# Feature tiles 32 bytes further on their line each, and the weights' parts in six separate buffers at different places

## The chip, the cores and the metric

One core of one Trainium2 chip runs the whole kernel. The metric is device time in microseconds: 953.28 us, the median of three runs (951.79, 953.28, 955.75). The engines are named as in the profile: PE multiplies matrices, PEld is its loading of the stationary operand, DVE and ACT are the vector and the scalar engine, SP issues the DMAs. Arrays lie in the on-chip memory with 128 partitions; an address below is a byte offset within a partition, the same in all partitions.

## The reference

One layer of a hybrid decoder trunk, for one sequence of 256 tokens and 2048 features (D), with a branch width of 4096 (E), all in float32:

```python
h = rmsnorm(x, norm_g);  mod = silu(c) @ ada_w + ada_b      # shift, scale, gate: 3 x 2048
h = h * (1 + scale) + shift
b, c_gate, v, g = split(h @ w_in, 4)                        # w_in: 2048 x 16384
u = causal_depthwise_conv(c_gate * v, conv_w)               # 3 taps
y = b * u * silu(g)
x = x + gate * (y @ w_out)                                  # w_out: 4096 x 2048
out = rmsnorm(x, final_g)
```

Nearly all the arithmetic is in `h @ w_in` (128 MiB of weights) and `y @ w_out` (32 MiB); `silu(c) @ ada_w` reads another 48 MiB.

## The kernel before, in words

**Two parts of each number.** A float32 product is made of three products of a shorter format (fp32r). Both operands are split: hi is the value rounded by ACT's cast (L191), lo is the rest, subtracted by DVE (L192). `split` (L187) does this for each raw block of weights that a DMA brings. A raw block, a hi block and a lo block take 8192 bytes of a partition each (SLOT = 2048 numbers), and each kind has three buffers that its pool hands out in turn. The tokens' features are split likewise: hT holds for each of 16 feature tiles k a row of 512 numbers, 256 tokens hi (`hh_`) and 256 tokens lo (`hl_`).

**Part 1 (`part`, L264; to about 406 us of the profile).** The first half of the branch channels, in four chunks by four quarters of w_in. While the conditioning vector's shift and scale are still being computed (`ada_piece`, L216, on DVE), matmuls begin with the feature tiles that are finished; `plan` (L41) sets that order, and a scheduler then places the instructions of all engines. For each feature tile k and each of four 128-channel columns there are three matmuls of 256 token columns: weights hi with features hi (L286), hi with lo (L291), lo with hi (L292). Each has its own load of stationary weights, a 128x128 block, so 3072 matmuls and 3072 loads. 85 blocks are split here.

**Part 2 (L365, about 407 to 762 us).** The second half: per feature tile and column one matmul of 512 columns (L382: weights hi with features hi and lo side by side) and one of 256 (L385: weights lo with features hi); 1024 of each, 64 blocks.

**Part 3 (L449, about 763 to 943 us).** y @ w_out. Now y is stationary (128 tokens of one channel tile, y hi or y lo) and the weights of w_out move, 512 columns: L427 (y hi, weights hi), L428 (y hi, weights lo), L429 (y lo, weights hi); 768 matmuls, 32 blocks. In the last quarter of the output, dc = 3, the matmuls of the second half of the tokens, po[1], with the last three blocks are put behind all of po[0] (the list `late`, L473 and L498), and the tail of the first half of the tokens (`gated`, L477, `finish`, L433: square, root, scale, store) runs beside them.

**Order of loads and matmuls on PE.** A matmul's stationary block is loaded while the matmul before it runs. So each matmul of the three parts reads its moving tile while the next matmul's weights are read from another place of the same memory.

**Small buffers.** The first group of ada_w pieces (four pieces, `at0`, L226) borrows two lo and two hi buffers. `gjunk` (L211, 512 bytes) takes the unused output of 32 small ACT sums (L249).

Of the kernel before, what the change touches and what calls it, by code (L numbers as in the profile page):

```python
# [8 lines left out]
F32 = mybir.dt.float32  # L9
F32R = mybir.dt.float32r  # L10
AF = mybir.ActivationFunctionType
ALU = mybir.AluOpType

P = 128
D = 2048
E = 4096
T = 256
KT = D // P
# [17 lines left out]
SLOT = 2048  # L36
ASLOT = 1024
# [51 lines left out]
def short_conv_layer(ctx: ExitStack, tc: tile.TileContext, x, c, norm_g, ada_w, ada_b, w_in, conv_w, w_out, final_g, out):  # L89
    nc = tc.nc  # L90
    PSUM = bass.MemoryType.PSUM

    const = ctx.enter_context(tc.tile_pool(name="const", bufs=1))
    adap = ctx.enter_context(tc.tile_pool(name="adap", bufs=2))
    wpool = ctx.enter_context(tc.tile_pool(name="wpool", bufs=2))
    psum = ctx.enter_context(tc.tile_pool(name="psum", bufs=6, space=PSUM))
    hpool = ctx.enter_context(tc.tile_pool(name="hpool", bufs=1, side="right"))
# [65 lines left out]

    hT = hpool.tile([P, KT, 2 * T], F32R, tag="big", name="hT")
    hh_ = hT[:, :, 0:T]
    hl_ = hT[:, :, T : 2 * T]
    xs = [slot([P, CT, T], f"xs{j}") for j in range(KT // CT)]
# [1 line left out]
    for k in range(0, KT, 2):  # L171
        tp = psum.tile([P, 2, T], F32, tag="sm", name="tp_x", bufs=2)
# [11 lines left out]
    shift = const.tile([P, KT], F32, tag="shift", name="shift")  # L184
    scale = const.tile([P, KT], F32, tag="scale", name="scale")

    def split(raw, n):  # L187

        hi = wpool.tile([P, SLOT], F32R, tag="hi", name="hi", bufs=3)
        lo = wpool.tile([P, SLOT], F32R, tag="lo", name="lo", bufs=3)  # L190
        nc.scalar.copy(hi[:, :n], raw[:, :n])  # L191
        nc.vector.tensor_tensor(out=lo[:, :n], in0=raw[:, :n], in1=hi[:, :n].bitcast(F32), op=ALU.subtract)  # L192
        return hi, lo
# [14 lines left out]


    acc = {}  # L210
    gjunk = const.tile([P, P], F32, tag="gjunk", name="gjunk")  # L211
    adas = ada_w[0].rearrange("(k p) (s f) -> p k s f", p=P, s=3)

    sums = {}
# [1 line left out]
    def ada_piece(k0, nk, piece):  # L216
        w = nk * P
        kk = ASLOT // (2 * w)
        if piece == 0:
            sums[k0] = adap.tile([P, 2, 2 * P], F32, tag="gv", name="gv")  # L220
        gv = sums[k0]

        turns = [gv[:, :, i * w : (i + 1) * w] for i in range(2 if k0 == 0 and nk == 1 else 1)]
        j = piece * kk
        if k0 == 0:
            at = wpool.tile([P, SLOT], F32, tag=("lo", "hi")[piece % 2], name="at0", bufs=3)[:, :ASLOT]  # L226
        else:
            at = adap.tile([P, ASLOT], F32, tag="at", name="at", bufs=4)
        at4 = at.rearrange("p (k s f) -> p k s f", k=kk, s=2)
        for s in range(2):  # L230
            nc.sync.dma_start(at4[:, :, s, :], adas[:, j : j + kk, s, k0 * P : k0 * P + w])  # L231
        for i in range(kk):
            c_k = silu_c[:, j + i : j + i + 1]
            g2 = turns[(j + i) % len(turns)]
            if j + i < len(turns):
                nc.vector.tensor_scalar_mul(g2, at4[:, i], c_k)
            else:
                nc.vector.scalar_tensor_tensor(out=g2, in0=at4[:, i], scalar=c_k, in1=g2, op0=ALU.mult, op1=ALU.add)  # L238
        if j + kk < KT:
            return  # L240
        if len(turns) == 2:
            nc.vector.tensor_tensor(out=turns[0], in0=turns[0], in1=turns[1], op=ALU.add)

        tp = psum.tile([P, 4, P], F32, tag="sm", name="tp_g", bufs=2)
        gs = const.tile([P, 4], F32, tag="gs", name="gs", bufs=2)
        for o in range(2 * nk):
            nc.tensor.transpose(tp[:, o, :], gv[:, o // nk, (o % nk) * P : (o % nk + 1) * P], ident)
        for o in range(2 * nk):
            nc.scalar.activation(gjunk, tp[:, o, :], AF.Copy, accum_out=gs[:, o : o + 1])  # L249
        ks = slice(k0, k0 + nk)  # L250
        nc.vector.tensor_tensor(out=scale[:, ks], in0=gs[:, nk : 2 * nk], in1=b_scale[:, ks], op=ALU.add)
        nc.vector.tensor_tensor(out=shift[:, ks], in0=gs[:, 0:nk], in1=b_shift[:, ks], op=ALU.add)
        nc.vector.scalar_tensor_tensor(
            out=scale[:, ks], in0=scale[:, ks], scalar=1.0, in1=gT[:, ks], op0=ALU.add, op1=ALU.mult
        )
        for k in range(k0, k0 + nk):
            hf = xs[k // CT][:, k % CT, :]
            nc.vector.tensor_scalar(
                out=hf, in0=hf, scalar1=scale[:, k : k + 1], scalar2=shift[:, k : k + 1], op0=ALU.mult, op1=ALU.add
            )  # L260
            nc.scalar.copy(hh_[:, k], hf)  # L261
            nc.vector.tensor_tensor(out=hl_[:, k], in0=hf, in1=hh_[:, k].bitcast(F32), op=ALU.subtract)
# [55 lines left out]
    for kind, *step in plan():  # L318
        if kind == "ada":
            ada_piece(*step)  # L320
        else:
            ch, k1 = step[0], step[3]
            part(*step)
            whole[ch] += k1 == KT
            if k1 == KT and whole[ch] == 4:
                mixed(ch)
# [40 lines left out]
    for ct in range(NS, NCT, 2):  # L367
        for q in QUARTERS:
            banks = [psum.tile([P, 2, T], F32, tag="mm", name="mm_b") for _ in range(2)]
            col = q * E + ct * P  # L370
            for kp in range(0, KT, KP):
# [5 lines left out]
                hi, lo = split(raw, SLOT)  # L377
                for m in range(2):
                    for i in range(KP):
                        k = kp + i  # L380
                        o = slice((i * 2 + m) * P, (i * 2 + m + 1) * P)
# [28 lines left out]
    big = hpool.tile([P, 4, D], F32, tag="big", name="big")  # L410
# [38 lines left out]
    for dc in range(4):  # L449
# [8 lines left out]
        for ep in range(n_ep):  # L458
# [11 lines left out]
            hi, lo = split(raw, SLOT)  # L470
# [55 lines left out]
```

## Time and profile before

| what | value |
|---|---|
| median of 3 runs | 953.28 us (951.79 to 955.75) |
| the profiled execution | 952.04 us, its span 950.2 us |
| granted TensorE clock, mean over the span | 0.99 |
| PE busy | 918.3 us, 97% of the span, 5963 matmuls |
| DVE busy | 681.4 us, 72% |
| ACT busy | 419.3 us, 44% |
| DMA | 227.51 MB, 239 GB/s in the mean |

The span is cut by line, engine and operation; a matmul's duration is longer than the distance to the next one, since they are pipelined. So the pace of PE is read from the number of matmuls in a stretch that has no idle time, not from their durations.

### The profile page before, as it was taken

How to read it: one execution, taken by the hardware profiler on the slowest of the kernel's cores; microseconds unless marked ns; L12 is line 12 of the kernel's file. 1: busy time of each engine (PE TensorE's matmuls, PEld its weight loads, DVE VectorE, ACT ScalarE, POOL GpSimd, SP SyncE). 2: the span in 40 equal slices, each digit the busy share in tenths (PEclk: the TensorE clock that was granted, in tenths of full speed). 3: DMA queues.
4: the chain of work that ended last, by engine and by line, in shares of the span. 5: the costliest groups of instructions: out<-in, count | busy, mean ns of one | idle time of the engine just before them, and what ended most of it. 6: DMA issues, size and time to landing. Idle time of an engine off the chain costs nothing.

```text
span 950.2 us, 14332 instructions
## 1 busy us (share of the span) xinstructions
PE 918.3 (97%) x5963; PEld 835.4 (88%) x5963; DVE 681.4 (72%) x789; ACT 419.3 (44%) x470; POOL 0.7 (0%) x6
## 2 busy tenths in 40 slices
PE   2799999999999999999999999999999999999996
PEld 2699999999999999988888888888888878888885
DVE  4799998999999998997465556555555654544882
ACT  6575343443435544444443444444444433343333
POOL 0000000000000000000000000000000000000000
PEclk9799999999999999999999999999999999999998
DMA  9999997999989787886665565566555685555542
GB/s 273 299 360 368 291 335 253 323 347 319 350 278 308 243 271 240 281 288 208 193 201 181 185 199 193 178 193 201 181 178 190 206 313 177 180 199 196 178 133 88
DMA packets 172048, 227.51 MB, mean 239 GB/s; under 512 B 5792, under 2 KB 112464, under 8 KB 171600
## 3 DMA queue, kind: packets, MB, share of 16 engines
q1 hardware_dynamic: 171984, 226.61, 72.9%
q8 instruction: 46, 0.75, 0.3%
q14 instruction: 18, 0.15, 0.0%
HBM read 224.49 MB, written 2.10 MB: 238 GB/s over the span
## 4 chain that ended last, share of the span: by engine, by line
PE 91%; DMA 4%; DVE 2%; issue 1%; SPq 1%; ACT 0%; ACTq 0%; DVEq 0%
PE mm_b L382 25%; PE mm_b L385 13%; PE mm_s L292 11%; PE mm_s L286 11%; PE mm_s L291 11%; PE mm_o L428 6%; PE mm_o L427 6%; PE mm_o L429 6%; DMA at<-in_ada_w_dram 2%; DMA raw_s<-in_sc_w_in_dram 2%; DVE lo L192 1%; DMA x<-in_x_dram 1%; DVE gv L238 1%; SPq L231 0%; PE ps_gate L362 0%
## 5 line engine op out<-in xcount | busy, mean ns | idle before, releaser
L382 PE MATMUL mm_b<-hT,hi 128*128 128x512 f32 x1024 | 355.2, 392 | 0.0
L286 PE MATMUL mm_s<-hT,hi 128*128 128x256 f32 x1024 | 286.9, 284 | 7.5 <-ACT hT L261 4.9
L291 PE MATMUL mm_s<-hT,hi 128*128 128x256 f32 x1024 | 287.7, 283 | 0.0
L385 PE MATMUL mm_b<-hT,lo 128*128 128x256 f32 x1024 | 285.4, 280 | 0.0
L292 PE MATMUL mm_s<-hT,lo 128*128 128x256 f32 x1024 | 283.6, 283 | 1.7 <-DVE lo L192 1.7
L192 DVE TENSOR_TENSOR lo<-raw,hi 128x2048 fp32r<-128x2048 f32 x64 | 146.6, 2291 | 128.4 <-ACT hi L191 128.4
L382 PEld LDWEIGHTS mm_b<-hT,hi 128*128 128x128 f32 x1024 | 192.0, 188 | 42.3 <-issue 0.2
L191 ACT CAST hi<-raw_s 128x2048 fp32r<-128x2048 f32 (+3 forms) x85 | 126.5, 1488 | 177.1 <-PE mm_s L291 128.6
L286 PEld LDWEIGHTS mm_s<-hT,hi 128*128 128x128 f32 x1024 | 194.4, 191 | 8.5 <-ACT hT L261 5.1
L291 PEld LDWEIGHTS mm_s<-hT,hi 128*128 128x128 f32 x1024 | 195.5, 191 | 0.2 <-issue 0.2
L292 PEld LDWEIGHTS mm_s<-hT,lo 128*128 128x128 f32 x1024 | 192.6, 191 | 2.6 <-DVE lo L192 2.4
L385 PEld LDWEIGHTS mm_b<-hT,lo 128*128 128x128 f32 x1024 | 192.3, 188 | 0.5 <-issue 0.2
L191 ACT CAST hi<-raw 128x2048 fp32r<-128x2048 f32 x64 | 122.4, 1912 | 158.0 <-PE mm_b L382 103.1
L192 DVE TENSOR_TENSOR lo<-raw_s,hi 128x2048 fp32r<-128x2048 f32 (+3 forms) x85 | 149.5, 1759 | 19.9 <-ACT hi L191 19.5
L192 DVE TENSOR_TENSOR lo<-raw_o,hi 128x2048 fp32r<-128x2048 f32 x32 | 73.3, 2290 | 67.0 <-ACT hi L191 67.0
L191 ACT CAST hi<-raw_o 128x2048 fp32r<-128x2048 f32 x32 | 61.2, 1913 | 103.8 <-PE mm_o L429 93.6
L428 PE MATMUL mm_o<-lo,y 128*128 128x512 f32 x256 | 101.7, 399 | 0.0
L427 PE MATMUL mm_o<-hi,y 128*128 128x512 f32 x256 | 101.0, 396 | 0.0
L429 PE MATMUL mm_o<-hi,y 128*128 128x512 f32 x256 | 100.1, 392 | 0.0
L238 DVE SCALAR_TENSOR_TENSOR gv<-at,silu_c,gv 128x512 f32<-128x512 f32 (+1 forms) x149 | 92.2, 639 | 3.8 <-DMA at<-in_ada_w_dram 3.0
L427 PEld LDWEIGHTS mm_o<-hi,y 128*128 128x128 f32 x256 | 48.1, 188 | 12.6 <-issue 0.2
L429 PEld LDWEIGHTS mm_o<-hi,y 128*128 128x128 f32 x256 | 48.1, 188 | 11.6
(84 smaller groups left out, 457.8 us busy)
## 6 DMA issues: line engine op xcount, KB each, us to landing
raw<-in_sc_w_in_dram SPq DMA_DIRECT2D x64, 1024.0 KB, 5.6
raw_s<-in_sc_w_in_dram SPq DMA_DIRECT2D x46, 1024.0 KB, 7.3
at<-in_ada_w_dram SPq DMA_DIRECT2D x128, 256.0 KB, 6.7
raw_o<-in_sc_w_out_dram SPq DMA_DIRECT2D x32, 1024.0 KB, 5.1
at_g<-in_ada_w_dram SPq DMA_DIRECT2D x32, 512.0 KB, 6.9
raw_s<-in_sc_w_in_dram SPq DMA_DIRECT2D x19, 512.0 KB, 5.4
raw_s<-in_sc_w_in_dram SPq DMA_DIRECT2D x7, 768.0 KB, 7.7
raw_s<-in_sc_w_in_dram SPq DMA_DIRECT2D x13, 256.0 KB, 4.4
```

The lines of the kernel that those rows point to most:

```text
L191: nc.scalar.copy(hi[:, :n], raw[:, :n])
L192: nc.vector.tensor_tensor(out=lo[:, :n], in0=raw[:, :n], in1=hi[:, :n].bitcast(F32), op=ALU.subtract)
L238: nc.vector.scalar_tensor_tensor(out=g2, in0=at4[:, i], scalar=c_k, in1=g2, op0=ALU.mult, op1=ALU.add)
L286: first = nc.tensor.matmul(dst, hi[:, o], hh, start=opens, stop=False, skip_group_check=True)
L291: nc.tensor.matmul(dst, hi[:, o], hl, start=False, stop=False, skip_group_check=True)
L292: nc.tensor.matmul(dst, lo[:, o], hh, start=False, stop=k == k1 - 1, skip_group_check=True)
L382: nc.tensor.matmul(banks[m].rearrange("p a t -> p (a t)"), hi[:, o], hT[:, k, :], start=k == 0, stop=False, skip_group_check=True)
L385: nc.tensor.matmul(banks[m][:, 0, :], lo[:, o], hh_[:, k], start=False, stop=k == KT - 1, skip_group_check=True)
L427: nc.tensor.matmul(po, yh, hi[:, o], start=opens, stop=False, skip_group_check=True)
L428: nc.tensor.matmul(po, yh, lo[:, o], start=False, stop=False, skip_group_check=True)
L429: nc.tensor.matmul(po, yl, hi[:, o], start=False, stop=ct == NCT - 1, skip_group_check=True)
```

## The change

Three places are edited. The row of a feature tile in hT becomes 520 numbers instead of 512, of which 512 are used: the tile k begins 2080 k bytes behind the first instead of 2048 k. The three hi and three lo buffers, until now two pools with three buffers in turn, become six pools of one buffer each, chosen by a count n of the splits: hi by n mod 3, lo by (n + n // 20) mod 3; four of them are 32 bytes longer, and so the buffers behind them begin 32 bytes further. The borrowed at0 buffers take the new names. To make room, gjunk goes, and the small ACT sums write their unused output over their own input.

```diff
--- before.py
+++ after.py
@@ -163,7 +163,8 @@
 
 
 
-    hT = hpool.tile([P, KT, 2 * T], F32R, tag="big", name="hT")
+
+    hT = hpool.tile([P, KT, 2 * T + 8], F32R, tag="big", name="hT")[:, :, 0 : 2 * T]
     hh_ = hT[:, :, 0:T]
     hl_ = hT[:, :, T : 2 * T]
     xs = [slot([P, CT, T], f"xs{j}") for j in range(KT // CT)]
@@ -184,10 +185,14 @@
     shift = const.tile([P, KT], F32, tag="shift", name="shift")
     scale = const.tile([P, KT], F32, tag="scale", name="scale")
 
+    n_split = [0]
+
     def split(raw, n):
 
-        hi = wpool.tile([P, SLOT], F32R, tag="hi", name="hi", bufs=3)
-        lo = wpool.tile([P, SLOT], F32R, tag="lo", name="lo", bufs=3)
+        i, j = n_split[0] % 3, (n_split[0] + n_split[0] // 20) % 3
+        n_split[0] += 1
+        hi = wpool.tile([P, SLOT + 8 * (i < 2)], F32R, tag=f"hi{i}", name=f"hi{i}", bufs=1)
+        lo = wpool.tile([P, SLOT + 8 * (j < 2)], F32R, tag=f"lo{j}", name=f"lo{j}", bufs=1)
         nc.scalar.copy(hi[:, :n], raw[:, :n])
         nc.vector.tensor_tensor(out=lo[:, :n], in0=raw[:, :n], in1=hi[:, :n].bitcast(F32), op=ALU.subtract)
         return hi, lo
@@ -208,7 +213,6 @@
 
 
     acc = {}
-    gjunk = const.tile([P, P], F32, tag="gjunk", name="gjunk")
     adas = ada_w[0].rearrange("(k p) (s f) -> p k s f", p=P, s=3)
 
     sums = {}
@@ -223,7 +227,9 @@
         turns = [gv[:, :, i * w : (i + 1) * w] for i in range(2 if k0 == 0 and nk == 1 else 1)]
         j = piece * kk
         if k0 == 0:
-            at = wpool.tile([P, SLOT], F32, tag=("lo", "hi")[piece % 2], name="at0", bufs=3)[:, :ASLOT]
+            j = piece // 2 % 3
+            at = wpool.tile([P, SLOT + 8 * (j < 2)], F32, tag=("lo", "hi")[piece % 2] + "012"[j], name="at0", bufs=1)[:, :ASLOT]
+            j = piece * kk
         else:
             at = adap.tile([P, ASLOT], F32, tag="at", name="at", bufs=4)
         at4 = at.rearrange("p (k s f) -> p k s f", k=kk, s=2)
@@ -246,7 +252,7 @@
         for o in range(2 * nk):
             nc.tensor.transpose(tp[:, o, :], gv[:, o // nk, (o % nk) * P : (o % nk + 1) * P], ident)
         for o in range(2 * nk):
-            nc.scalar.activation(gjunk, tp[:, o, :], AF.Copy, accum_out=gs[:, o : o + 1])
+            nc.scalar.activation(tp[:, o, :], tp[:, o, :], AF.Copy, accum_out=gs[:, o : o + 1])
         ks = slice(k0, k0 + nk)
         nc.vector.tensor_tensor(out=scale[:, ks], in0=gs[:, nk : 2 * nk], in1=b_scale[:, ks], op=ALU.add)
         nc.vector.tensor_tensor(out=shift[:, ks], in0=gs[:, 0:nk], in1=b_shift[:, ks], op=ALU.add)
```

What this does to the places, in bytes modulo 128, as the built programs lay them out (all steps within a buffer are multiples of 512 there, apart from the new 2080):

| buffer | before | changed |
|---|---|---|
| feature tiles hh and hl of tile k | 96 for all k | 96 + 32 k: 96, 0, 32, 64 in turn |
| hi buffers 0, 1, 2 | 64, 64, 64 | 96, 32, 64 |
| lo buffers 0, 1, 2 | 64, 64, 64 | 64, 0, 64 |
| y blocks | 96 | 96 |

For each matmul the difference of the moving tile's place and that of the block being loaded meanwhile, modulo 128, over the built programs' order on PE:

| difference | part 1 before | changed | part 2 before | changed | part 3 before | changed |
|---|---|---|---|---|---|---|
| 0 | 0 | 776 | 0 | 517 | 0 | 175 |
| 32 | 3070 | 760 | 2046 | 507 | 0 | 88 |
| 64 | 0 | 770 | 0 | 521 | 0 | 160 |
| 96 | 2 | 766 | 2 | 503 | 767 | 344 |

The number of instructions on each engine stays what it was. Their order moves a little in part 1 and at the end. One place is DVE at the 20th to 22nd split (part 1, about 100 to 110 us of the profile). Before, a split took the lo buffer of the third split ahead of it; with (n + n // 20) mod 3 the splits 20 and 21 (and 40, 41, 60, 61 and so on, counted from 0) take the buffer of the split but one before. The rows before, where lo_1225 and lo_1252 belong to the splits 20 and 21, gv and at to the conditioning, and the brackets name what an instruction waits for:

```order
L192 TENSOR_TENSOR lo_1225<-raw_s_1222,hi_1224 128x512 [waits DMAHW2_49]
L238 SCALAR_TENSOR_TENSOR gv_1058<-at_1242,silu_c_95,gv_1058 128x512 [waits DMAHW4_49,DMAHW3_49,DVE_49]
L262 TENSOR_TENSOR hT_116<-xs1_118,hT_116 128x256 [waits Activation_49] x2
L300 TENSOR_TENSOR acc03_369<-mm_s_1115,acc03_369 128x512 [waits PE_49]
L300 TENSOR_TENSOR acc03_369<-mm_s_1116,acc03_369 128x512 [waits PE_49]
L238 SCALAR_TENSOR_TENSOR gv_1058<-at_1242,silu_c_95,gv_1058 128x512 [waits DVE_49]
L238 SCALAR_TENSOR_TENSOR gv_1058<-at_1323,silu_c_95,gv_1058 128x512 [waits DMAHW6_49,DMAHW5_49,DVE_49]
L192 TENSOR_TENSOR lo_1252<-raw_s_1249,hi_1251 128x2048 [waits DMAHW1_49,Activation_49]
```

and now, with lo0_1224 and lo1_1251 for the same two splits:

```order
L306 TENSOR_TENSOR acc03_368<-mm_s_1114,acc03_368 128x512 [waits PE_49]
L306 TENSOR_TENSOR acc03_368<-mm_s_1115,acc03_368 128x512 [waits PE_49]
L197 TENSOR_TENSOR lo0_1224<-raw_s_1221,hi2_1223 128x512 [waits DMAHW2_49]
L244 SCALAR_TENSOR_TENSOR gv_1057<-at_1241,silu_c_95,gv_1057 128x512 [waits DVE_49]
L244 SCALAR_TENSOR_TENSOR gv_1057<-at_1322,silu_c_95,gv_1057 128x512 [waits DMAHW6_49,DMAHW5_49,DVE_49]
L244 SCALAR_TENSOR_TENSOR gv_1057<-at_1322,silu_c_95,gv_1057 128x512 [waits DVE_49]
L197 TENSOR_TENSOR lo1_1251<-raw_s_1248,hi0_1250 128x2048 [waits DMAHW1_49,PE_49,Activation_49]
```

The subtraction of split 20 has moved behind the sums into acc, and that of split 21 now waits for PE as well: for the last matmul that reads the lo part of split 19, whose buffer it takes.

The other place is the end of PE's work. The last three splits are 178 to 180, and 180 takes the lo buffer of 178, which the late matmuls of po[1] still read. The rows before, where mm_o_8268 is po[0], mm_o_8269 is po[1], and hi_8468 and lo_8469 belong to split 180:

```order
L427 MATMUL mm_o_8268<-hi_8468,y15_4637 128x512
L428 MATMUL mm_o_8268<-lo_8469,y15_4637 128x512
L429 MATMUL mm_o_8268<-hi_8468,y15_4637 128x512
L429 MATMUL mm_o_8269<-hi_8449,y12_4634 128x512
L427 MATMUL mm_o_8269<-hi_8449,y12_4634 128x512
L428 MATMUL mm_o_8269<-lo_8450,y12_4634 128x512
```

and now, where mm_o_8267 is po[0] and mm_o_8268 is po[1], and hi0_8467 and lo0_8468 belong to split 180:

```order
L433 MATMUL mm_o_8267<-hi0_8467,y15_4636 128x512
L434 MATMUL mm_o_8267<-lo0_8468,y15_4636 128x512
L435 MATMUL mm_o_8267<-hi0_8467,y15_4636 128x512
L434 MATMUL mm_o_8268<-lo0_8468,y14_4635 128x512
L435 MATMUL mm_o_8268<-hi0_8467,y14_4635 128x512
L433 MATMUL mm_o_8268<-hi0_8467,y14_4635 128x512
```

Behind the last matmul of po[0] 22 matmuls of po[1] were left; now the ones with the splits 178 and 179 come ahead of it, and 11 are left. Between the last matmul that reads the lo part of split 178 and the first one that reads that of split 180 stand 14 others.

## The prediction

> **What bounds the kernel now.** I read the page's shares first, then the chain of waits, then the windows of the three parts, and last single matmuls in the timeline.
>
> ```profile
> span 950.2 us, 14332 instructions
> PE 918.3 (97%) x5963; PEld 835.4 (88%) x5963; DVE 681.4 (72%) x789; ACT 419.3 (44%) x470; POOL 0.7 (0%) x6
> PE 91%; DMA 4%; DVE 2%; issue 1%; SPq 1%; ACT 0%; ACTq 0%; DVEq 0%
> ```
>
> PE is busy 97% of the span and 91% of the chain that ended last is PE's own work. So the time moves with the pace of PE's matmuls, or with a new wait ahead of one. The windows below lie one in each part (columns: stretch, its length, then busy time and count of each engine, the granted clock, DMA), and the fourth lies in the opening, where the clock was still halved.
>
> ```profile
> 57.00:320.00 263.00, 262.52 (x2214) 262.32 (x2214) 240.72 (x312) 114.17 (x145) 0.00 (x0) 1.00 0.95 316
> 407.00:762.00 355.00, 355.00 (x2047) 312.20 (x2046) 216.25 (x217) 158.49 (x160) 0.00 (x0) 1.00 0.61 196
> 764.00:942.00 178.00, 178.00 (x764) 143.21 (x763) 101.14 (x67) 65.74 (x52) 0.00 (x0) 1.00 0.53 182
> 30.00:33.00 3.00, 3.00 (x16) 3.00 (x15) 3.00 (x8) 2.28 (x4) 0.00 (x0) 0.50 0.79 252
> ```
>
> PE is never idle in them, so length over count is the pace: 263/2214 = 118.8 ns for a 256-column matmul in part 1; 355/2047 = 173.4 ns in part 2, or 346.8 ns for its pair of 512 and 256 columns; 178/764 = 233.0 ns for 512 columns in part 3. How much of that is the bare passing of columns is told by the half-clock stretch:
>
> ```profile
> 30.06 0.41 PE L292 MATMUL mm_s<-hT,lo 128*128 128x256 f32 x1
> ...
> 32.84 0.41 PE L292 MATMUL mm_s<-hT,lo 128*128 128x256 f32 x1
> ```
>
> From 30.06 to 32.84 there are 13 steps, 213.8 ns each at a granted clock of 0.50, so 256 columns should pass in 106.9 ns at full clock and 512 in 213.8 ns. What is paid above that, per matmul, is 118.8 - 106.9 = **11.9 ns** in part 1, (346.8 - 320.7)/2 = **13.1 ns** in part 2, 233.0 - 213.8 = **19.2 ns** in part 3. Over 3072, 2048 and 768 matmuls it is 36.6, 26.8 and 14.7 us, together 78 us of the span. This sum is the only stock from which the change can gain, and it pays once for each load of a stationary block, whatever the matmul's width: at full clock the load starts with the matmul ahead of it and overlaps it.
>
> ```profile
> 433.03 0.28 PE L385 MATMUL mm_b<-hT,lo 128*128 128x256 f32 x1
> 433.03 0.19 PEld L382 LDWEIGHTS mm_b<-hT,hi 128*128 128x128 f32 x1
> 433.15 0.39 PE L382 MATMUL mm_b<-hT,hi 128*128 128x512 f32 x1
> 433.15 0.19 PEld L385 LDWEIGHTS mm_b<-hT,lo 128*128 128x128 f32 x1
> ```
>
> **The change, part by part.** *The places.* The table of the change gives for each load the difference, modulo 128 bytes, between the moving tile and the block loaded meanwhile. Before, it is 32 in parts 1 and 2 (price 11.9 and 13.1 ns) and 96 in part 3 (19.2 ns). After, each of 0, 32, 64, 96 has a quarter of parts 1 and 2, and 175, 88, 160 and 344 of 767 in part 3. If the price hangs on the difference, two of four are known from the rows above. Of 64, only the transposes of the sums tell something (L247: identity and sums lie 64 apart):
>
> ```profile
> L247 PE MATMUL tp_g<-ident,gv x32: 270/272/329, 22.0 to 265.4; 128*128 128x128 f32 x32
> 265.07 0.60 PE L247 MATMUL tp_g<-ident,gv 128*128 128x128 f32 x4
> L362 PE MATMUL ps_gate<-gacc,ones 128*128 128x512 f32 x8 | 4.1, 593 | 0.0
> L382 PE MATMUL mm_b<-hT,hi 128*128 128x512 f32 x1024 | 355.2, 392 | 0.0
> ```
>
> Four of them take 0.60 us, the last one 0.272 of it, so they start (0.60 - 0.272)/3 = 109.3 ns apart. Their columns are full float32, and such columns take about twice an fp32r column: 512 of them last 593 ns where 512 of the others last 392, 201 ns more, near the 213.8 of 512 steps. So 128 of them need 106.9 ns, and the price there is 2.4 ns. Since their moving columns pass at half the pace, I take twice that, 5 ns, for difference 64. Of 0 no row speaks: I take the middle between nothing and the dearest known price, 9.6 ns. Both are bounded by 0 below (the stock can't be more than used up) and by 19.2 above, the dearest row.
>
> Part 1: (9.6 + 11.9 + 5 + 19.2)/4 = 11.4 ns, 0.5 less than now, times 3072 = -1.5 us. Part 2: (9.6 + 13.1 + 5 + 19.2)/4 = 11.7, 1.4 less, times 2048 = -2.8 us. Part 3, with 12.5 for difference 32: (175 x 9.6 + 88 x 12.5 + 160 x 5 + 344 x 19.2)/767 = 13.3, 5.9 less, times 768 = -4.5 us. Together **-8.8 us**. With both unknown prices at 0 the prices are 7.8, 8.1 and 10.0 and the sum is -12.6 - 10.2 - 7.0 = -29.8 us; with both at 19.2 they are 17.4, 17.7 and 18.4 and it is +16.8 + 9.4 - 0.6 = +25.6 us. DVE is no new bound: it is busy 240.72 of 263 us in the window of part 1, so 8% could be gained there before it binds.
>
> *The lo buffers' new turn.* At the splits 20, 40, 60 and so on, and at the ones behind them, DVE waits for PE's use of the split but one before. In parts 2 and 3 the split between has 16 pairs, 16 x 346.8 ns = 5.5 us, or more of PE's work, against 2.3 us for the subtraction, so PE does not wait; in part 1 the shortest cover but one is a block of 24 matmuls, 24 x 118.8 ns = 2.8 us. The exception is split 21, because split 20 has 12 matmuls only. Its subtraction now:
>
> ```profile
> 104.24 2.28 DVE L192 TENSOR_TENSOR lo<-raw_s,hi 128x2048 fp32r<-128x2048 f32 x1
> ```
>
> It must now start after the last matmul with the lo part of split 19, and the first matmul that reads its result comes 17 places behind that one: 17 x 118.8 ns = 2.0 us, against 0.28 us until that matmul ends, 2.28 us and about 0.15 us of signals. **+0.7 us** of PE waiting. Behind DVE's wait stand sums for acc and for the conditioning; DVE lags some 3 us there; for the lag I add nothing, since DVE has 22 us to spare in the window of part 1 and the conditioning's sums are needed only groups later.
>
> *The end.* The first half's tail ran beside 22 matmuls of the second half, now beside 11.
>
> ```profile
> 937.79 0.60 ACT L484 ACTIVATE big<-mm_o 128x512 f32<-128x512 f32 x1 [9.72 <-PE mm_o L429]
> 940.32 1.34 ACT L446 ACTIVATE big<-big,fs 128x512 f32<-128x512 f32 x2 [0.23 <-DVE fs L437]
> 942.92 0.60 ACT L484 ACTIVATE big<-mm_o 128x512 f32<-128x512 f32 x1 [1.26 <-PE mm_o L429]
> ```
>
> ACT works on the first tail from 937.79 to 941.66, 3.87 us, and the second one's square starts at 942.92, 5.13 us behind the first. With 11 matmuls, 11 x 233 = 2.57 us, ACT is still in the first tail for 1.3 us when the second is due: **+1.3 us**. The subtraction of split 180, which now waits for the last use of split 178, has 14 matmuls, 3.3 us, for its 2.3: hidden.
>
> *At nothing:* the start and gjunk. The first hi block takes the buffer of the second at0 piece; that piece's sums are the third to sixth of the twelve below, done by 14.30 + 6 x 0.40 = 16.7, and the cast comes at 18.45. The 32 small sums of L249 now write over their input; if each took twice its 279 ns, ACT, 44% busy, would hide all but the first pair, 0.6 us.
>
> ```profile
> 14.30 4.83 DVE L238 SCALAR_TENSOR_TENSOR gv<-at,silu_c,gv 128x256 f32<-128x256 f32 x12
> 18.45 0.62 ACT L191 CAST hi<-raw_s 128x512 fp32r<-128x512 f32 x1 [0.87 <-DMA raw_s<-in_sc_w_in_dram]
> L249 ACT ACTIVATE gjunk<-tp_g 128x128 f32<-128x128 f32 x32 | 8.9, 279 | 8.8 <-PE tp_g L247 8.2
> ```
>
> Sum: -8.8 + 0.7 + 1.3 = -6.8 us on the profiled execution's own 952.04 us gives 945.2. The median of the runs shown, 953.28, lies 1.2 above that execution, so **946 us**.
>
> **The rivals.** *(A) Place does not matter.* The 12 to 19 ns may belong to the swap of stationary blocks itself. For it: parts 1 and 2 have nearly one price although half of part 2's matmuls are twice as wide. Against it: part 3 pays half as much again with the same kind of load, and the half-clock stretch shows no more than columns. Then only the two waits remain: 952.04 + 2.0 + 1.2 = **955 us**. The Trainium skill speaks for this one: SBUF — State Buffer, section "Who interferes with whom", gives PE two independent read ports, one for the moving operand and one for the weight load, and says "PE and ACT never wait on anyone". By that rule the two reads can't meet, and the change could only bring the two waits; no row here says whether the ports are what the price comes from.
>
> *(B) The weights' own place sets the price.* The two known prices go with the difference, but just as well with where the loaded block lies: 64 (a multiple of 64) costs 11.9 to 13.1, 96 (32 past one) costs 19.2. The hi buffers 0 and 1 move to 96 and 32, both 32 past; the lo buffers stay on multiples of 64, y stays. Then two thirds of the hi loads turn dear: part 1, 2048 x 2/3 x 7.3 ns = 10.0 us; part 2, 1024 x 2/3 x 6.1 = 4.2 us; part 3 nothing. 952.04 + 14.2 + 2.0 + 1.2 = **969 us**. Nothing in the trace separates this from the forecast; against it stands only that the transposes, too, load from a multiple of 64, at 2.4 ns. It decides for slower from a surcharge of (4.8 - 2.0)/2048 = 1.4 ns on those loads.
>
> **How the numbers follow.** The forecast, that the difference counts and the new mix is cheaper, gets 0.48; its own range is 925 (both unknown prices 0) to 951. (A) gets 0.24, (B) 0.28; the dear end of the mix, 981 us, is counted with (B), since the two differ only in which loads turn dear. About 0.5%, 4.8 us, is what a measurement of this kernel can tell from no change: 948.5 to 958. Faster: 0.44, nearly all of the forecast. Same: 0.27, its rest, most of (A), and (B) at a small surcharge. Slower: 0.29, (B) and the case that (A)'s waits are longer than worked out. The range, 925 to 971, leaves out the mix far beyond either end.
>
> **What would show it.** Right: length over count in the same windows gives about 118.3, 172.0 and 227 ns; within part 1 the pace changes with k mod 4; one PE wait of about 0.7 us near 109 us, and the second square of L490 (L484 before) starts right behind the first tail. For (A) the three paces stay at 118.8, 173.4 and 233. For (B) matmuls ahead of a load from hi buffer 0 or 1 are about 7 ns longer, those ahead of hi buffer 2 or any lo buffer are not, and part 3 stays. The forecast is wrong if part 3, where it sees the largest gain per load, does not get faster.

## The result, and the profile after

The changed kernel is slower: 957.95 us in the median of 5 runs (955.91 to 958.63) against 953.28 us in 5 runs of the kernel before (951.79 to 955.75). The ratio is 1.0051, 95% interval 1.0034 to 1.0069. The profiled execution took 958.52 us with a span of 956.7 us, 6.5 us more span than before. The shares and the chain of waits of the changed kernel read almost as before:

```profile
span 956.7 us, 14339 instructions
...
PE 921.1 (96%) x5963; PEld 835.7 (87%) x5963; DVE 682.2 (71%) x789; ACT 418.8 (44%) x470; POOL 0.7 (0%) x6
...
PE 89%; DMA 5%; DVE 3%; ACT 1%; issue 1%; SPq 1%; ACTq 0%; DVEq 0%
```

PE is busy 2.8 us longer for the same 5963 matmuls, and its share of the chain fell by two points, which went to others that it waits for. So two things have to be found: a slower pace, and waits. The starts of the stages, from the timeline of each trace, say where (us from the span's start):

| | before | changed | cost of the stage |
|---|---|---|---|
| part 1 begins | 27.34 | 27.53 | +0.2 |
| part 2 begins | 406.76 | 409.49 | +2.5 |
| part 3 begins | 763.11 | 769.45 | +3.6 |
| last matmul begins | 942.49 | 947.67 | -1.2 |
| end of the span | 950.23 | 956.74 | +1.3 |

For the pace, windows that lie inside part 2 and part 3 in every kernel of this study (412 to 762 and 774 to 942 us; PE's busy time and its count of matmuls come behind the length). First the kernel before, then the changed one:

```profile
412.00:762.00 350.00, 350.00 (x2019) 307.78 (x2018) 211.25 (x209) 156.68 (x159) 0.00 (x0) 1.00 0.61 195
774.00:942.00 168.00, 168.00 (x721) 135.15 (x720) 94.43 (x61) 61.98 (x48) 0.00 (x0) 1.00 0.50 169
```

```profile
412.00:762.00 350.00, 350.00 (x1998) 305.35 (x1998) 208.35 (x205) 153.58 (x156) 0.00 (x0) 1.00 0.60 193
774.00:942.00 168.00, 168.00 (x726) 135.99 (x725) 96.36 (x61) 60.73 (x44) 0.00 (x0) 1.00 0.54 184
```

PE is never idle and the granted clock is 1.00 in all four. In part 2, 350/2019 x 2 = 346.7 ns for a pair before, 350/1998 x 2 = 350.4 ns now: 3.6 ns x 1024 pairs = +3.7 us. In part 3, 168/721 = 233.0 ns before, 168/726 = 231.4 now: -1.6 ns x 768 = -1.2 us. From the starts of single matmuls the paces are 346.7 and 350.2 ns, 233.4 and 231.8 ns, and in part 1, without the waits, 118.63 and 118.25 ns. So the pace gained 1.1 us in part 1 and 1.2 in part 3, and lost 3.6 in part 2, where the forecast had a gain of 2.8. The gain in part 1 is not shown to come from the places: the kernel with the lo turn alone, whose places are those of before, has 118.1 ns there.

The wait at split 21 and the end came as forecast. The grouped waits of PE for the lo parts of part 1, before and changed (line, what was waited for, us in total, times, longest):

```profile
PE mm_s L292 <- DVE lo L192: 1.7, 3, 0.7
```

```profile
PE mm_s L298 <- DVE lo L197: 3.9, 5, 1.3
```

Split 21 in the changed kernel's timeline, DVE and then PE:

```profile
108.69 2.29 DVE L197 TENSOR_TENSOR lo<-raw_s,hi 128x2048 fp32r<-128x2048 f32 x1 [2.28 <-PE mm_s L298]
```

```profile
110.18 0.28 PE L297 MATMUL mm_s<-hT,hi 128*128 128x256 f32 x1
111.03 0.40 PE L298 MATMUL mm_s<-hT,lo 128*128 128x256 f32 x1 [0.57 <-DVE lo L197]
```

DVE stands 2.28 us for the matmul whose buffer it wants, and PE's next start comes 0.85 us behind the one ahead of it instead of 0.12: 0.73 us. And the end, on ACT:

```profile
945.55 0.60 ACT L490 ACTIVATE big<-mm_o 128x512 f32<-128x512 f32 x1 [12.22 <-PE mm_o L435]
...
948.08 1.33 ACT L452 ACTIVATE big<-big,fs 128x512 f32<-128x512 f32 x2 [0.23 <-DVE fs L443]
949.32 0.57 ACT L490 ACTIVATE big<-mm_o 128x512 f32<-128x512 f32 x1
```

The second square (949.32) has no idle time ahead of it: it stands right behind the first tail, although the last matmul started at 947.67. From that start to the end of the span it is 9.07 us, before it was 7.74: +1.33 us.

One wait of 0.88 us was not in the forecast. It is behind split 60, one of the splits that take the buffer of the split but one before. In the new order of DVE three more sums of the gate (gacc) stand ahead of its subtraction, and the last two of these sums wait 4.02 us for a DMA, so the subtraction starts at 287.43 us and PE waits for it:

```profile
285.97 1.54 DVE L365 SCALAR_TENSOR_TENSOR gacc<-at_g,silu_c,gacc 128x512 f32<-128x512 f32 x2 [4.02 <-DMA at_g<-in_ada_w_dram]
287.43 2.28 DVE L197 TENSOR_TENSOR lo<-raw_s,hi 128x2048 fp32r<-128x2048 f32 x1
```

```profile
289.77 0.39 PE L298 MATMUL mm_s<-hT,lo 128*128 128x256 f32 x1 [0.88 <-DVE lo L197]
```

Before, the same subtraction starts at 281.02 us, and PE doesn't wait for it:

```profile
281.02 2.29 DVE L192 TENSOR_TENSOR lo<-raw_s,hi 128x2048 fp32r<-128x2048 f32 x1
```

The 2.5 us of part 1 as a whole can't be given to the change from two profiled executions: four kernels of this study have the same part 1 in instructions and places (the kernel before and three of the experiments that change only part 2 or 3), and their part 2 begins at 406.76, 406.29, 409.38 and 409.31 us. Their paces without waits, 118.6 to 118.8 ns, make only 0.5 us of that; the rest is waits, above all one: PE stands 2.6 us for the cast of a hi block in each of the early two, and 4.0 and 4.1 us in the late two.

### The profile page after: what moved, and what is told of

Its sections match the earlier page's. It is cut to its first block, busy times and chain, and to the rows that moved or that the text cites. A ratio compares the mean times of both kernels' runs of the same rounds, so it can differ in the third digit from the quotient of the medians.

```text
span 956.7 us, 14339 instructions
## 1 busy us (share of the span) xinstructions
PE 921.1 (96%) x5963; PEld 835.7 (87%) x5963; DVE 682.2 (71%) x789; ACT 418.8 (44%) x470; POOL 0.7 (0%) x6
## 4 chain that ended last, share of the span: by engine, by line
PE 89%; DMA 5%; DVE 3%; ACT 1%; issue 1%; SPq 1%; ACTq 0%; DVEq 0%
PE mm_b L388 25%; PE mm_b L391 13%; PE mm_s L298 11%; PE mm_s L297 11%; PE mm_s L292 11%; PE mm_o L433 6%; PE mm_o L435 6%; PE mm_o L434 6%; DMA raw_s<-in_sc_w_in_dram 2%; DVE lo L197 1%; DMA at<-in_ada_w_dram 1%; DMA at_g<-in_ada_w_dram 1%; DMA x<-in_x_dram 1%; DVE gv L244 1%; ACT hi L196 1%
## 5 line engine op out<-in xcount | busy, mean ns | idle before, releaser
L434 PEld LDWEIGHTS mm_o<-lo,y 128*128 128x128 f32 x256 | 48.1, 188 | 11.6 <-issue 0.2
L433 PEld LDWEIGHTS mm_o<-hi,y 128*128 128x128 f32 x256 | 48.0, 188 | 11.4 <-issue 0.2
```

Of the source, the lines that this page charges most:

```text
L433: nc.tensor.matmul(po, yh, hi[:, o], start=opens, stop=False, skip_group_check=True)
L434: nc.tensor.matmul(po, yh, lo[:, o], start=False, stop=False, skip_group_check=True)
```

## The experiments

The theory on trial: the price of 12 to 19 ns above bare columns hangs on the difference of places, and the change picked a bad mix. The rivals: the price belongs to the swap of stationary blocks whatever the place, and only the waits cost; the weights' own place sets it; and, formed after the result, that the price follows the widths of the matmuls, and place only shifts it a little. All ratios are against runs of the kernel before on the same chip.

| experiment | median, us | before, us | ratio (95% interval) |
|---|---|---|---|
| lo turn alone | 954.41 | 952.33 | 1.0021 (1.0007 to 1.0036) |
| all new places, old turn | 954.50 | 952.33 | 1.0027 (1.0015 to 1.0038) |
| feature tiles' step alone | 954.90 | 952.33 | 1.0036 (1.0024 to 1.0048) |
| buffers' places alone | 952.75 | 952.33 | 1.0009 (0.9996 to 1.0022) |
| weights moved by 32 bytes | 956.15 | 952.03 | 1.0044 (1.0028 to 1.0060) |
| weights moved by 64 | 960.26 | 952.03 | 1.0085 (1.0068 to 1.0102) |
| weights moved by 96 | 956.46 | 952.03 | 1.0047 (1.0028 to 1.0066) |
| part 2 all 512 wide | 1076.74 | 951.94 | 1.1312 (1.1245 to 1.1378) |
| part 3 in halves | 957.58 | 951.94 | 1.0057 (1.0034 to 1.0079) |
| part 3, 512 and 256 in turn | 952.26 | 952.61 | 0.9996 (0.9984 to 1.0007) |

None of them beats the kernel before.

### The lo turn alone, and the places alone

The kernel before with six named buffers and the new turn of lo, all places as before:

```diff
+    n_split = [0]
     def split(raw, n):
-        hi = wpool.tile([P, SLOT], F32R, tag="hi", name="hi", bufs=3)
-        lo = wpool.tile([P, SLOT], F32R, tag="lo", name="lo", bufs=3)
+        i, j = n_split[0] % 3, (n_split[0] + n_split[0] // 20) % 3
+        n_split[0] += 1
+        hi = wpool.tile([P, SLOT], F32R, tag=f"hi{i}", name=f"hi{i}", bufs=1)
+        lo = wpool.tile([P, SLOT], F32R, tag=f"lo{j}", name=f"lo{j}", bufs=1)
```

> The kernel before with the change's turn of the buffers alone: six buffers of one tile each, lo by (n + n // 20) mod 3, no byte of padding, hT and gjunk as before. Every place modulo 128 is that of before; the order of instructions on every engine is that of the change. Theory W (the change's loss comes from the turn: its waits and the later end of po[0]): about 953.3 + 2.0 to 3.5, so 955 to 957, with the last matmul to end of the program 1.3 us longer than before, a PE wait near 110 us, and the paces of before (118.6, 346.7 a pair, 233.4 ns). Theory P (the places cost, the turn is nearly free): 953 to 954.

The changed kernel with the old turn, all places as changed:

```diff
-        i, j = n_split[0] % 3, (n_split[0] + n_split[0] // 20) % 3
+        i, j = n_split[0] % 3, n_split[0] % 3
```

> The changed kernel with lo by n mod 3: all of the change's places, but the order of instructions and the waits of before. Theory W: the tail and the waits come back to before, and the places are worth nothing: about 953 to 955. Theory P: the pace of part 2 stays at the 350.2 ns a pair that the changed kernel's trace shows (346.7 before), so part 2 keeps its +3.6 us, less some 2 us that parts 1 and 3 win: 955 to 957. The end from the last matmul on is 7.7 us in both.

Measured: the turn alone costs 0.21%, 2.1 us, the places alone 0.27%, 2.2 us, and 1.0021 x 1.0027 = 1.0048 against 1.0051 for both. So the two halves of the change add, and both are losses. The turn alone ends 9.07 us behind its last matmul, as the changed kernel does, and its paces in parts 2 and 3 are those of before (windows of the turn alone):

```profile
412.00:762.00 350.00, 350.00 (x2018) 307.81 (x2017) 209.72 (x207) 156.40 (x158) 0.00 (x0) 1.00 0.61 194
774.00:942.00 168.00, 168.00 (x722) 135.19 (x721) 95.35 (x59) 58.47 (x43) 0.00 (x0) 1.00 0.51 176
```

Its subtraction of split 60 starts as late as in the changed kernel, at 287.51 us, but PE arrives there later and doesn't wait.

With the old turn the end is 7.71 us, and the paces are those of the changed kernel (windows of the places alone):

```profile
412.00:762.00 350.00, 350.00 (x1997) 305.38 (x1996) 207.85 (x207) 155.17 (x158) 0.00 (x0) 1.00 0.60 193
774.00:942.00 168.00, 168.00 (x728) 136.31 (x727) 95.96 (x62) 60.98 (x47) 0.00 (x0) 1.00 0.52 175
```

From the starts of the stages in its trace part 2 takes 3.8 us more than before and part 3 1.4 less, +2.4 us, which is the measured +2.2. So the loss of the places is part 2's pace; its part 1, 0.8 us shorter, lies within what part 1 differs by itself.

### The feature tiles alone, and the buffers alone

```diff
-    hT = hpool.tile([P, KT, 2 * T], F32R, tag="big", name="hT")
+    hT = hpool.tile([P, KT, 2 * T + 8], F32R, tag="big", name="hT")[:, :, 0 : 2 * T]
```

(and without gjunk, as in the change; weights and turn as before)

> The kernel before with the 32-byte step of the feature tiles alone (and the small sums' output over their input); hi and lo buffers all at 64 modulo 128, the turn of before. If a price belongs to the difference of places, part 2 shows four prices by k mod 4, and part 3, where nothing moved, stays at 233.4 ns. If it is the jump of the moving tile's place from one matmul to the next that costs, part 2 is at or above 350 ns a pair, as in the changed kernel, though all weights lie at one place. If place is indifferent: 346.7 ns and 953 us.

The changed kernel's six buffers with their longer four, the old turn, and the feature tiles 2048 bytes apart as before (without gjunk too):

```diff
+        i, j = n_split[0] % 3, n_split[0] % 3
+        hi = wpool.tile([P, SLOT + 8 * (i < 2)], F32R, tag=f"hi{i}", name=f"hi{i}", bufs=1)
+        lo = wpool.tile([P, SLOT + 8 * (j < 2)], F32R, tag=f"lo{j}", name=f"lo{j}", bufs=1)
```

> The kernel before with the six different places of the buffers alone: hT rows of 512 numbers as before, lo by n mod 3. Within one split all loads of a kind have one place, and it changes from split to split. If a price belongs to the difference, each split of part 2 has a pace of its own by its hi and lo buffer, and part 3 has the changed kernel's 231.8 ns or so. If it is the jump of the moving tile that costs, part 2 stays at 346.7 ns. If place is indifferent: 953 us.

The windows of parts 2 and 3, first of the feature tiles alone, then of the buffers alone:

```profile
412.00:762.00 350.00, 350.00 (x1995) 304.70 (x1994) 207.53 (x206) 154.74 (x158) 0.00 (x0) 1.00 0.60 194
774.00:942.00 168.00, 168.00 (x721) 135.18 (x721) 95.11 (x59) 60.09 (x45) 0.00 (x0) 1.00 0.51 175
```

```profile
412.00:762.00 350.00, 350.00 (x2001) 306.31 (x2000) 210.25 (x209) 154.05 (x157) 0.00 (x0) 1.00 0.60 194
774.00:942.00 168.00, 168.00 (x727) 136.34 (x726) 96.12 (x60) 60.77 (x46) 0.00 (x0) 1.00 0.53 181
```

A pair takes 350.9 ns and 349.8 ns. Either edit by itself brings part 2 to the slower pace, and the two together (350.4) are no worse than one. Part 3, where the feature tiles are not read, stays at 721 matmuls in its window with the feature tiles alone and has 727 with the buffers alone, so its small gain is the weights' places. The buffers alone are therefore the mildest, +0.09%, not to be told from no change; the feature tiles' step, which has nothing to give in part 3, is the costliest single edit, +0.36%.

Of the two theories in these expectations, neither came in whole. That the moving tile's jump from one matmul to the next costs would have left part 2 at 346.7 ns with the buffers alone. That each difference has its price would have shown four prices by k mod 4 with the feature tiles alone; the trace repeats only every eight pairs, from 347 to 359 ns. With the buffers alone each split does have a pace of its own: by the starts in its timeline the pairs of a split take 351.9, 349.6 and 347.3 ns for n mod 3 of 0, 1 and 2, again and again. The last of these has every place as before, and it is the cheapest.

### One difference for all: the weights moved by 32, 64 and 96 bytes

A mix can hide what each difference does. Here one small constant ahead of the buffers is made longer, so that all weights' buffers move together and all differences of a part are equal. The raw blocks and the conditioning's buffers behind it move along, hT and the y blocks stay, and no instruction changes:

```diff
-    warm = const.tile([P, 1], F32, tag="warm", name="warm")
+    warm = const.tile([P, 16], F32, tag="warm", name="warm")[:, 0:1]   # then 24, then 32
```

> The kernel before with everything on the left side of the memory 32 bytes further (one small constant is padded): weights at 96 instead of 64 modulo 128, hT and y stay at 96, the order of instructions is that of before. All differences are 0, in all parts. Difference theory with the changed kernel's rows for difference 0: part 2 at 232.1 + 116.7 = 348.8 ns a pair, part 3 at 230.8 ns, about 953.3 + 2.1 - 2.0 = 953. The prediction's guess for difference 0 (9.6 ns a load): 940 us. Weights' own place (B of the prediction): hi and lo loads at 96 cost as in part 3, parts 1 and 2 slower by 22 and 12 us: 988 us. Place indifferent: paces of before within the spread that part 1 shows by itself (117.3 to 120.0), 951 to 956.

> As the run before this, but 64 bytes further: weights at 0 modulo 128. Differences: 96 in parts 1 and 2, 32 in part 3, so the two known differences change places. Difference theory: parts 1 and 2 pay 19.2 ns a load, part 3 pays 12.5: 953.3 + 22 + 12 - 5 = 983 us by the prices of before; by the changed kernel's rows part 2 at 234.7 + 118.5 = 353.2 ns a pair (+6.7 us) and part 3 at 229.1 (-3.3 us): 957. Weights' own place: all loads on a multiple of 64, paces of before: 953. Place indifferent: 951 to 956.

> As the run before this, but 96 bytes further: weights at 32 modulo 128. Differences: 64 in all three parts. The prediction's guess for 64 (5 ns a load): 953.3 - 21 - 17 - 11 = 904 us. By the changed kernel's rows part 2 at 231.8 + 118.6 = 350.3 ns (+3.7 us), part 3 at 233.6: 957. Weights' own place: as at 96, 988 us. Place indifferent: 951 to 956.

The windows of parts 2 and 3 with the weights moved by 32, by 64 and by 96 bytes:

```profile
412.00:762.00 350.00, 350.00 (x1993) 306.38 (x1992) 208.71 (x207) 154.60 (x158) 0.00 (x0) 1.00 0.60 193
774.00:942.00 168.00, 168.00 (x724) 136.23 (x723) 95.66 (x60) 60.45 (x45) 0.00 (x0) 1.00 0.52 179
```

```profile
412.00:762.00 350.00, 350.00 (x1998) 304.86 (x1997) 210.28 (x212) 154.70 (x157) 0.00 (x0) 1.00 0.61 195
774.00:942.00 168.00, 168.00 (x718) 135.06 (x718) 98.21 (x63) 60.84 (x44) 0.00 (x0) 1.00 0.55 187
```

```profile
412.00:762.00 350.00, 350.00 (x1988) 304.83 (x1987) 206.01 (x202) 154.51 (x158) 0.00 (x0) 1.00 0.60 192
774.00:942.00 168.00, 168.00 (x722) 135.61 (x721) 94.58 (x62) 61.20 (x48) 0.00 (x0) 1.00 0.50 171
```

Paces in ns from the starts of single matmuls, waits left out, with the difference that each part has:

| weights moved by | part 1, 256 columns | part 2, a pair | part 3, 512 columns |
|---|---|---|---|
| 0 (before) | 118.63 (diff. 32) | 346.7 (32) | 233.4 (96) |
| 32 | 118.66 (0) | 351.0 (0) | 232.4 (0) |
| 64 | 119.98 (96) | 350.1 (96) | 234.3 (32) |
| 96 | 117.08 (64) | 352.2 (64) | 233.3 (64) |
| changed kernel, mixed | 118.25 | 350.2 | 231.8 |

Above bare columns (106.9, 320.7 and 213.8 ns) that is 10.2 to 13.1 ns a load in part 1, 13.0 to 15.8 in part 2, and 18.6 to 20.5 in part 3. Difference 0 costs 15.2 ns in part 2 and 18.6 in part 3, where the forecast guessed 9.6; difference 64 costs 15.8 and 19.5, where it took 5 from the transposes; and difference 32, cheap in part 2, is the dearest in part 3. So the place moves the price by 2 to 3 ns, and it doesn't make part 3 dearer than part 2. The prices that the expectations had read off the changed kernel's mix (348.8, 353.2 and 350.3 ns for part 2) did not come in either. Since hT and y stay, these three shifts change the weights' own place and the difference together and can't tell which of the two counts; it isn't the weights' place alone, since the feature tiles' step slowed part 2 with the weights unmoved. In part 2 the place of before is the cheapest of the four: the other three cost 3.4 to 5.5 ns a pair, 3.5 to 5.6 us, and the four mixes measured there cost 3.1 to 4.2 ns by their windows. The rival of the weights' own place is out at the price that it was given, since moving all weights to 96 (the first shift) would have cost it 7.3 ns x 3072 = 22 us in part 1 alone, and part 1 stayed at 118.66.

The shift by 96 has one number that can't be relied on: part 1's 117.08 ns comes from a profiled execution of 953.04 us, while the other three of that kernel took 956.28 to 956.75.

### What makes 13 ns in part 2 and 19 in part 3

If not the place, then what? The parts differ in the widths that follow each other: 512 and 256 in turn in part 2, 512 behind 512 in part 3. First, part 2 with both matmuls 512 wide, at its own place (difference 32):

```diff
-                        nc.tensor.matmul(banks[m][:, 0, :], lo[:, o], hh_[:, k], start=False, stop=k == KT - 1, ...)
+                        nc.tensor.matmul(banks[m].rearrange("p a t -> p (a t)"), lo[:, o], hT[:, k, :], start=False, stop=k == KT - 1, ...)
```

> The kernel before, its places untouched, with one edit in part 2: the matmul of weights lo (L385) moves all 512 columns of the feature tile instead of 256, so that both matmuls of a pair are 512 wide, as in part 3. It adds the product of the two lo parts, which the reference's sum also contains. Every difference of places stays 32. What is asked: the price above the passing of columns is 13 ns a load in part 2 and 19 in part 3; does that contrast belong to the place, to the load, or to the width? If each load has its price by the part's places and whatever the width (13.0 ns, the mean of part 2 before), a pair takes 2 x (213.8 + 13.0) = 453.6 ns, +106.9 ns a pair, and the time is 952 + 1024 x 0.1069 = about 1061.5 us. If the price goes with the width, and in part 2 is 15.4 ns for 512 columns and 10.6 for 256 (229.2 and 117.5 ns from start to start), the pair takes 458.4 ns: 1066.5 us. If any stretch of 512-column matmuls alone pays what part 3 pays (19.5 ns), the pair takes 466.6 ns: 1075 us.

Second, part 3 with 256 behind 256, at its own place (difference 96):

```diff
-            nc.tensor.matmul(po, yh, hi[:, o], ...)
-            nc.tensor.matmul(po, yh, lo[:, o], ...)
-            nc.tensor.matmul(po, yl, hi[:, o], ...)
+            for c in range(2):
+                b = po[:, c * 256 : (c + 1) * 256]
+                o = slice(i * 512 + c * 256, i * 512 + (c + 1) * 256)
+                nc.tensor.matmul(b, yh, hi[:, o], ...)
+                nc.tensor.matmul(b, yh, lo[:, o], ...)
+                nc.tensor.matmul(b, yl, hi[:, o], ...)
```

> The kernel before, with one edit in part 3: each of the 768 matmuls of 512 columns is made as two of 256 columns, first the three products of the one half, then those of the other. So there are 1536 loads of the same y blocks instead of 768, the columns moved and all places modulo 128 bytes are as before (difference 96). If the price is paid for each load (19.5 ns, part 3 before), a half takes 106.9 + 19.5 = 126.4 ns, and the time is 952 + 1536 x 0.1264 - 768 x 0.2333 = about 967 us. If the price goes with the width, as part 2's 10.6 ns for 256 columns and 15.4 for 512 hint, a half takes 117.5 to 118.6 ns (parts 2 and 1 before) and the time is 953.3 to 955 us. If columns simply pass 9% slower than counted at the half clock, and no price hangs on loads, two halves take what one whole took, 116.6 ns each, and the time stays 952 us.

Third, part 3 with 512 and 256 in turn:

```diff
+            nc.tensor.matmul(po, yh, hi[:, o], ...)
+            nc.tensor.matmul(po[:, 0:256], yl, hi[:, o0], ...)
+            nc.tensor.matmul(po, yh, lo[:, o], ...)
+            nc.tensor.matmul(po[:, 256:512], yl, hi[:, o1], ...)
```

> The kernel before, places untouched, part 3 in the widths of part 2: for each channel tile a matmul of 512 columns (y hi, weights hi), one of 256 (y lo, first half of weights hi), one of 512 (y hi, weights lo), one of 256 (y lo, second half of weights hi); the same columns with four loads in place of three. The difference of places stays about that of part 3 (96). If the price goes with the widths that follow each other, as part 2 before shows for them (346.7 ns for 512 and 256 in turn, 26 ns above their columns, against 233.3 for 512 behind 512 and 120.0 for 256 behind 256), the four take 693.4 ns against 700.0 now: 256 x -6.6 ns = -1.7 us, about 950 us. If each width has its own price whatever is beside it (233.3 and 120.0 ns in part 3), the four take 706.6 ns: +1.7 us, 954 us. If the place of part 3 (96) makes a pair dear, by the 3.4 ns that the shift to 96 cost part 2's pair, 700.1 ns: no change.

One window each: part 2 of the first, part 3 of the second and of the third.

```profile
410.00:872.00 462.00, 462.00 (x1972) 371.16 (x1971) 211.31 (x205) 153.07 (x155) 0.00 (x0) 1.00 0.45 145
```

```profile
766.00:942.00 176.00, 176.00 (x1467) 175.87 (x1466) 100.23 (x64) 62.68 (x46) 0.00 (x0) 1.00 0.55 185
```

```profile
766.00:942.00 176.00, 176.00 (x1006) 153.24 (x1005) 100.66 (x66) 65.19 (x51) 0.00 (x0) 1.00 0.54 185
```

Part 2 all 512 wide: 462/1972 = 234.3 ns, 20.5 above its columns, nearest to the third of the expectations. At unchanged places the price of part 2's loads rose into the range of part 3's. Part 3 in halves: 176/1467 = 120.0 ns, 13.1 above its columns: at unchanged places the price fell into the range of part 1's. None of the three expectations had this; the nearest, 117.5 to 118.6 ns, was too low. The third: 176/1006 x 2 = 349.9 ns for a pair (by the starts in the timeline, any 16 successive groups of four take 700.0 ns each in the mean, the first few apart), 14.6 ns a load. With difference 96 part 2 had 350.1 (the shift by 64), so at the same widths and the same difference the two parts agree to 0.2 ns. The other two runs have such partners as well, and they agree as closely: part 2 all 512 wide (difference 32) with part 3 of the shift by 64 (also 32), 234.3 and 234.3 ns; part 3 in halves (96) with part 1 of the shift by 64 (also 96), 120.0 and 119.98 ns. In these three pairs the stationary blocks lie at different places, so widths and difference together gave the pace. Of the three expectations for this run the one with the place in it came in: what the widths in turn would save, part 3's place takes back, and the time stays.

So the widths set most of the price and the place the last 2 to 3 ns: in the mean of a part 256 behind 256 pays 10 to 13 ns, 512 behind 512 18.6 to 20.5, in turn 26 to 31.5 for the two. It is neither a price for each load (part 3 in halves has twice the loads, and the price summed over the part went from 768 x 19.5 = 15.0 us to 1536 x 13.1 = 20.1 us) nor a share of the columns (then the halves would have stayed at 116.7 ns).

## Why the prediction failed, step by step

The measured 957.95 us lies in the stated range of 925 to 971, but the forecast was 946, faster by 7 us, and the kernel became slower by 4.7.

**What bounds the kernel** held: PE's pace, the waits ahead of it and the later end made the difference, at a full granted clock in the windows of parts 2 and 3. One reading was slightly off: in part 1's window PE is busy 262.52 of 263.00 us, so the pace without waits is 118.6 ns and not 118.8.

**The step that failed is "If the price hangs on the difference, two of four are known from the rows above".** The rows gave 12 to 13 ns in parts 1 and 2 and 19 in part 3, and the difference of places was one of several things in which these parts differ. The widths were another, and in the same timeline: the prediction counted the price "once for each load of a stationary block, whatever the matmul's width", while part 2's timeline had 117.5 ns behind its 256 columns and 229.2 behind its 512, 10.6 and 15.4 ns. Part 2 at full width and part 3 in halves show that the contrast goes with the widths at unchanged places. What hung on that step fell with it: the price of 5 ns for difference 64, taken from transposes of 128 columns in another format, measures 10.2, 15.8 and 19.5 ns in the three parts, and the middle of 9.6 for difference 0 measures 11.8, 15.2 and 18.6.

**The three terms of the places**: part 1 forecast -1.5 us, its pace gave -1.1; part 2 forecast -2.8, measured +3.6; part 3 forecast -4.5, measured -1.2. The wrong sign is in part 2. There the bounds of the prediction reached from -10.2 to +9.4 us, so that the measured value lay inside them; the value chosen between them had the wrong sign. Part 1's -1.1 is luck as far as the record goes, since the turn alone gains as much without any new place.

**The waits** that the prediction named were right: split 21 forecast +0.7 us, measured 0.73; the end forecast +1.3, measured 1.33; the turn by itself +2.1 us (0.7 to 3.4 by the interval) against a sum of 2.0. What it put at nothing, the splits 40, 60 and 80 of part 1, failed at split 60: the cover was counted from the buffer's release, and the wait of 0.88 us came from the order of DVE's work. One more wait for a lo part looks new, at 178.95 us:

```profile
178.95 0.38 PE L298 MATMUL mm_s<-hT,lo 128*128 128x256 f32 x1 [1.29 <-DVE lo L197]
```

Most of it is not the turn's: the kernel before waits 0.5 us at the same matmul, near 176.3 us, and two kernels with the part 1 of before wait 1.0 and 1.1 us there (part 3 in halves, and 512 and 256 in turn).

The terms as measured, -1.1 + 3.6 - 1.2 of the paces and 0.7 + 0.9 + 1.3 of the waits and the end, make +4.2 us; the medians differ by 4.7.

**At nothing**: the start and gjunk are in order, part 1 begins 0.2 us later.

**The rivals.** That place doesn't matter, 955 us, was the nearest, and its waits are what the turn costs; its paces did not stay, though: part 2's rose by 3.5 ns a pair, which is the other half of the loss. The rule of the Trainium skill that stood behind it (SBUF — State Buffer, section "Who interferes with whom": PE's two read ports are independent) has its limit here: places moved the price by no more than 3 ns a load, but moving the weights by 32 bytes with the same instructions costs 0.44%, which that rule does not foresee; whether the two reads ever meet is not shown. The weights' own place, 969 us, is refuted at its price of 7.3 ns by the shift.

**What would show it.** "Wrong if part 3 does not get faster" was the wrong thing to look at: part 3 got faster, by 1.6 ns instead of 5.9, and the kernel slower, since part 2 has the more matmuls.

What stays open: what the price is, and whether any of it is paid at half the clock, because the 106.9 ns of bare columns are themselves taken from the half-clock steps. These are the same with the new places; the changed kernel's opening has 13 steps of 213.8 ns between these two rows, as before:

```profile
30.04 0.41 PE L297 MATMUL mm_s<-hT,hi 128*128 128x256 f32 x1
...
32.82 0.41 PE L297 MATMUL mm_s<-hT,hi 128*128 128x256 f32 x1
```

And no law was found by which the prices of the differences make up that of a mix: the mean of the four constant paces is 350.0 ns in part 2, near the mixed kernel's 350.2, but in part 3, weighted by the table of differences, it is 233.2 where the mix has 231.8.

## What to carry to other kernels

A contrast between two stages has as many possible causes as the stages have differences; before a forecast rests on one of them, look in the same rows for another that explains it, here the width of the matmuls, which stood in the timeline. When an edit changes places and a buffer's turn together, cost the turn first: who waits for the buffer before last, and what runs beside the tail, could be worked out to 0.1 us, while the places could not. A buffer's turn also changes the scheduler's order, though, and that brought a third wait that nobody had counted. And where a kernel already runs at one constant place, a shift of every buffer by 32, 64 and 96 bytes costs one line each and tells what the other places cost; for a mix it is a guide only, good to 0.2 ns in part 2 and 1.4 ns off in part 3.

## What was unexpected of the hardware

**The pace stands still at a few values.** In part 1 of the kernel before, with the same places throughout, three stretches of 34 us without a wait:

```profile
92.00:126.00 34.00, 34.00 (x292) 34.00 (x291) 32.08 (x43) 14.76 (x16) 0.00 (x0) 1.00 0.97 313
130.00:164.00 34.00, 34.00 (x286) 34.00 (x285) 30.48 (x43) 10.72 (x10) 0.00 (x0) 1.00 0.82 264
330.00:364.00 34.00, 34.00 (x289) 34.00 (x288) 32.86 (x42) 17.70 (x17) 0.00 (x0) 1.00 0.86 279
```

These have 292, 286 and 289 matmuls (two or three of them already under way at the edge), and the starts are 117.33, 120.00 and 118.67 ns apart in the mean of every 60 successive ones, for hundreds of matmuls; a change came only behind an interruption of the stream. Over 3072 matmuls the outer two values lie 8 us apart, more than the whole change made. What selects the value was not found. With the weights moved by 32 bytes all long stretches of part 1 run at 118.67 ns, with 64 all at 120.00, and with 96 they stand at 113.33 or 117.78.

**A few tens of bytes are worth up to 0.85%.** Moving all weights by 64 bytes, with the same instructions in the same order, cost 8.2 us in the median: 4.3 us until part 2 begins, 3.4 in part 2, 0.7 in part 3, by the stages of its trace.
